# A decoder layer on one core: the first block sum of each group moved from VectorE to an accumulating DMA, weight blocks put into any free slot, and attention heads begun while the value projection still runs

## The chip, the cores and the metric

The kernel runs on one core of a Trainium2 chip. The metric is the device time of one execution in microseconds (us), less being better: the median of three runs of the kernel before is 1005.34 us.

The core's engines work side by side, each through its own list of instructions in order, and wait for one another on semaphores: TensorE multiplies matrices (PE in the profile; PEld is its loading of weights), VectorE (DVE) and ScalarE (ACT) do elementwise work, GpSimd (POOL) does a little of it and issues some transfers, and SyncE (SP) issues the rest.

## What is computed

The reference is one residual layer with four causal token mixers, for a sequence of 256 tokens and a width of 2048. Cut to what matters:

```python
h = rms_norm(x, norm_w)
p = h @ w_in                       # 2048 x 17492: z, gates, q/k/v of four mixers, indexer
o = [dsa(...), fox(...), diff(...), dilated(...)]   # four heads of 128 each
for b in range(4):
    y = o[b].reshape(1, 256, 512) * silu(z[b])
    term = sigmoid(gate[b]) * (y @ w_branch[b])     # 512 x 2048
    merged = term if b == 0 else merged + term
out = rms_norm(x + merged @ w_out, final_norm_w)    # 2048 x 2048
```

All of it is in float32. The mixers differ in their logits: dsa attends to the 64 best keys of an indexer with 16 small heads, fox adds cumulative forget gates, diff subtracts two softmax maps, and dilated merges three windows. Each head ends in a product of its probabilities with v.

## The kernel before

**Numbers.** TensorE gets each float32 operand as a high and a low part. For a weight block, ScalarE writes the high part (`whi`, `split_hi`, L194) and VectorE the low part (`wlo`, `split_lo`, L207), each for half a block at a time, and `three` multiplies high by high, low by high and high by low (L365 to L367). ScalarE runs up to `HI` = 8 such halves ahead of the products, VectorE up to `LO` = 6.

**Blocks.** Weights come from HBM in blocks of 512 rows by 512 columns (1 MB, `Raw`, tile `raw`), into six slots. Each block has a slot written down in the program and each slot its own queue (`waiting`): `free` loads the slot's next block when the low half of the last product that reads it has been written. The loads are issued on SyncE's queue.

**Groups.** `seven` multiplies two 512-column blocks of the output by a scheme with seven products, in place of eight, over the first half of the rows, and four plain products (c1a, c1b, c2a, c2b) over the second. It is called 17 times: for each of the four branches q with k, z with v, and two groups of gates; and once for the output projection (`Out`). A group's units are P1 to P7 and the four plain ones, a P unit of 12 matmuls of 128x512, a c unit of 24. Four sums of weight blocks belong to a group, made in place by `plus` (VectorE, 128x2048, L174): B12+B11, then +B22, then B21 plus that, and B11 minus that. The first is made ahead of P5, the first unit of the group (fourth in the first group and the last, which are `late`). A function `plus_dram`, which adds a block from HBM by a transfer on POOL's queue, stands in the file and isn't called.

**Order.** `units` lists all units, and the main loop writes them out one after the other: the splits that lie ahead, the unit's matmuls, its evictions (`post`), and then, at intervals, one step of every thread that is active (`run_threads`). Threads are generators for what isn't a weight product: the indexer, the transposes of q and k (`qk_thread`) and of z, and the attention heads (`head_thread`, `diff_thread`). A step is taken when the summed `cost` of units reaches `pace`: 17, or 14 in branch 2; here 12 for a P unit and 24 for a c unit. What the threads issue stands in the engines' lists at that place. The branches come in the order 3 (dilated), 2 (diff), 0 (dsa), 1 (fox). A branch's heads begin with its values in place: they start behind the unit c1b of the group of z and v, which waits for `qk`, `fox`, `const` and, for dsa, `index`. In a head, logits go through a softmax (L802), `transposed` turns the probabilities (tiles `ptp` in PSUM, `pt` in SBUF, copied by ScalarE at L813), and a product with v gives `o` (L855) or `od` (L886). A branch's product with `w_branch` (`ps_b`) waits for its four heads.

Of the kernel before, what the change touches and what calls it, by code (L numbers as in the profile page):

```python
# [20 lines left out]
KC = D // P  # L21
# [52 lines left out]
class Raw:  # L74


    def __init__(self, slot, src, k0, nk, c0, n):
        self.slot, self.src, self.k0, self.nk, self.c0, self.n = slot, src, k0, nk, c0, n
        self.tile = self.then = None
# [31 lines left out]
def body(ctx: ExitStack, tc, x, norm_w, w_in, fox_b_f, lq1, lk1, lq2, lk2, subln_w,  # L111
# [227 lines left out]
    def tok_units(src, c0, act, slots, evict, name, need=(), start=()):  # L339

        st = {}
        units = []
        nk = 4 * len(slots)
        for i, slot in enumerate(slots):
# [5 lines left out]
            units.append(Unit(Raw(slot, src, 4 * i, 4, c0, 512), mm))  # L350
# [27 lines left out]
    def T_units(c0, evict, name, slots, ps_of=main_ps):  # L378
# [3 lines left out]
        for k0 in range(0, KC, 4):  # L382
# [11 lines left out]
            units.append(Unit(Raw(slots[k0 // 4], w_in, k0, 4, c0, 512), mm))  # L394
# [40 lines left out]
    def seven(src, c1, c2, base, ev, name, need={}, start=(), late=False, s0=0):  # L435
# [5 lines left out]
        B11, B12 = Raw(0, src, s0, 4, c1, 512), Raw(1, src, s0, 4, c2, 512)  # L441
        B21, B22 = Raw(3, src, s0 + 4, 4, c1, 512), Raw(2, src, s0 + 4, 4, c2, 512)
# [30 lines left out]
        def c(k0, c0, two):  # L473
            return Unit(Raw(4 + k0 // 4 % 2, src, k0, 4, c0, 512), plain(k0, two))
# [16 lines left out]
        u1 = unit("P1", B11, product("Y", whole(0, s0), True), [read(ev.p1, "Y")])  # L491
        u3 = unit("P3", B22, product("Z", form(0, 4), not late))
        second = [lambda: plus(B12, B22), lambda: free([B22])]
        fourth = [lambda: plus(B21, B12), lambda: free([B12])]
        u6 = unit("P6", B12, product("Y", form(0, 0)), [read(ev.u2, "Y")])
        u7 = unit("P7", B11, product("Y", form(1, 0)), [read(ev.u3, "Y")], frees=[B11],
                  pre=[lambda: plus(B11, B12, ALU.subtract)])
        u2 = unit("P2", B21, product("X", whole(0, s0 + 4), True))
        u4 = unit("P4", B21, product("Y", whole(1, s0 + 4)), frees=[B21])
        c2a, c2b = c(p0, c2, "ZW"), c(p0 + 4, c2, "ZW")  # L500
        c1a, c1b = c(p0, c1, "XY"), c(p0 + 4, c1, "XY")
        c2a.need += need.get("c2a", ())
        c1b.need += need.get("c1b", ())
        c1b.post += [read(ev.c11, "X", True), read(ev.c21, "Y", True)]
        c1b.start += start
        if late:
            u5.after += second[:1]
            u3.after += second[1:]
            u6.after += fourth
            u1.cost = u2.cost = 24  # L510
            u7.post += [read(ev.c12, "Z", True), read(ev.c22, "W", True)]
            return [c2a, u1, u2, u5, u3, u6, c2b, u7, c1a, u4, c1b]
        u6.pre += second
        u2.after += fourth
        c2b.post += [read(ev.c12, "Z", True)]
        u2.post += [read(ev.c22, "W", True)]
        return [u5, u1, u3, c2a, u6, c2b, u7, u2, c1a, u4, c1b]

    class Tok:


        def __init__(self, dst, s1, s2, late=False):
            self.dst, self.s1, self.s2, self.late = dst, s1, s2, late

        def p1(self, ps):
            if self.late:
                self.d1, self.d2 = self.dst()
            nc.scalar.activation(self.d1[:, 0], ps, AF.Copy, scale=self.s1[:, 0:1])

        def p5(self, ps):  # L530
            if self.late:
                nc.scalar.activation(self.d2[:, 1], ps, AF.Copy, scale=self.s2[:, 1:2])
            else:
                self.d1, self.d2 = self.dst()
# [7 lines left out]
        def u3(self, ps):  # L542
            if self.late:
                nc.vector.scalar_tensor_tensor(self.d2[:, 1], ps, self.s2[:, 1:2],  # L544
                                               self.d2[:, 1], op0=ALU.mult, op1=ALU.subtract)
            else:
                nc.scalar.activation(self.d2[:, 1], ps, AF.Copy, scale=self.s2[:, 1:2])  # L547
# [36 lines left out]
    def qkvz_units(b, off, scale, start):  # L584
# [36 lines left out]
        def z_thread():  # L621
# [209 lines left out]

    def head_thread(b, h):
        if h == 0:
            V["yT"] = big.tile([P, 4, 2, S], F32R, name="yT", tag="y")
        for _ in range(2 * h):
            yield
# [11 lines left out]
        scaled(e, r)  # L848
        yield
# [9 lines left out]
    def diff_thread(b, h):  # L859
        if h == 0:  # L860
            V["yT"] = big.tile([P, 4, 2, S], F32R, name="yT", tag="y")
        for _ in range(2 * h):
            yield
# [15 lines left out]
        yield  # L879
        yield  # L880
        pt = transposed(e0)
        yield
# [73 lines left out]
    def branch_units(b, n):  # L956
        def ev(ps):
# [6 lines left out]
            elif n == 0:  # L964
                for i in range(2):
                    load_m(i)
        units = tok_units(w_branch[b], n * 512, lambda k: (V["yT"][:, k, 0], V["yT"][:, k, 1]),
                         ((2, 0, 1, 3) if b == LAST else (2, 4, 3, 5))[n:n + 1], ev,
                         "ps_b", need=[f"att{b}"] if n == 0 else [],
# [98 lines left out]
    def out_units(n, slots):  # L1068
        if n == 2:
# [3 lines left out]
            return tok_units(w_out, n * 512, m_act, slots, ev, "ps_o")  # L1073
# [22 lines left out]
        units = [Unit(Raw(slots[i], w_out, 4 * i, 4, n * 512, 512), mm) for i in range(4)]  # L1096
# [7 lines left out]
    misc = Unit(Raw(3, w_in, 0, KC, ((O_IK, 80), (O_FF, 4)), 84), misc_mm,  # L1104
                start=[("index", misc_thread), ("const", const_thread)])
    misc.post.append(lambda: ev_misc(misc))
    units = T_units(O_IQ, lambda ps: ev_iq(ps, 0), "ps_iq", (0, 1, 2, 3))
    units[3].start += [rms_thread]
    units += T_units(O_IQ + 512, lambda ps: ev_iq(ps, 1), "ps_iq", (4, 0, 1, 2), ps_of=att_ps)
# [170 lines left out]
```

## Time and profile before

| what | value |
|---|---|
| median of 3 runs | 1005.34 us (1004.07 to 1007.09) |
| the profiled execution | 1004.6 us, of which the span of its instructions 1002.8 |
| TensorE busy | 959.9 us, 96% of the span |
| VectorE busy | 852.9 us, 85% |
| ScalarE busy | 626.3 us, 62% |
| GpSimd busy | 50.2 us, 5% |
| mean granted clock of TensorE | 0.985 of full speed |
| moved by DMA | 195.81 MB, 195 GB/s on average |

A stretch of the span in which an engine is idle costs nothing if that engine isn't the one that the others wait for. TensorE's busy share is the first thing to look at here; its ends are modelled, so 96% isn't 96% of its best. A granted clock under 1 means that TensorE ran a part of that stretch at 1.2 GHz in place of 2.4.

### The profile page before, as it was taken

The numbers are of one execution on the slowest core, as the hardware profiler recorded it, in microseconds if no ns is written. First come the engines' busy times: TensorE is split into PE (matmuls) and PEld (weight loads), VectorE is DVE, ScalarE is ACT, GpSimd is POOL, SyncE is SP. The second block draws the span as 40 slices with busy tenths as digits, with TensorE's granted clock in tenths as the row PEclk, the third lists the DMA queues.
The fourth block names the chain that finished last, engine by engine and source line by source line (L and its number), as shares of the span: only waits on it lengthen the run. The fifth ranks groups of instructions, "written<-read, shape, count | busy, mean of one in ns | idle before, by whom it ended". The sixth has DMA issues, their size and how long they took to land.

```text
span 1002.8 us, 12075 instructions
## 1 busy us (share of the span) xinstructions
PE 959.9 (96%) x4443; PEld 790.4 (79%) x4443; DVE 852.9 (85%) x985; ACT 626.3 (62%) x828; POOL 50.2 (5%) x67
## 2 busy tenths in 40 slices
PE   9997898999999999889999999999999999999896
PEld 8876686878888887668888887788888878888676
DVE  5898899989788987789799899887998989779982
ACT  5847464796655656685456667864666787544551
POOL 2010000000000000020100000001000000010130
PEclk9999899999999999899999999999999999999998
DMA  9936355555766555337786655577756465866232
GB/s 318 298 134 196 124 168 167 169 168 184 278 225 228 197 168 168 126 126 238 223 232 202 218 168 168 168 262 208 236 201 210 164 210 187 309 232 238 86 125 84
DMA packets 100043, 195.81 MB, mean 195 GB/s; under 512 B 7811, under 2 KB 10021, under 8 KB 99600
## 3 DMA queue, kind: packets, MB, share of 16 engines
q1 hardware_dynamic: 96240, 181.06, 53.5%
q0 software_dynamic: 3712, 13.98, 5.3%
q8 instruction: 35, 0.57, 0.2%
q14 instruction: 24, 0.20, 0.1%
q10 hardware_dynamic: 32, 0.01, 0.0%
HBM read 186.61 MB, written 8.41 MB: 194 GB/s over the span
## 4 chain that ended last, share of the span: by engine, by line
PE 78%; DVE 13%; issue 4%; ACT 3%; DMA 1%; POOL 0%; ACTq 0%; POOLq 0%; DVEq 0%; SPq 0%
PE ps_g L365 9%; PE ps_g L367 9%; PE ps_g L366 9%; DVE wlo L207 6%; PE ps_zv L367 5%; PE ps_zv L365 5%; PE ps_zv L366 5%; PE ps_qk L365 5%; PE ps_qk L366 5%; PE ps_qk L367 5%; PE ps_iq L370 3%; PE ps_b L367 3%; PE ps_b L365 3%; PE ps_b L366 3%; DVE raw L174 3%
## 5 line engine op out<-in xcount | busy, mean ns | idle before, releaser
L194 ACT ACTIVATE whi<-raw 128x1024 fp32r<-128x1024 f32 (+1 forms) x439 | 448.1, 1051 | 221.3 <-DVE raw L174 70.1
L207 DVE TENSOR_TENSOR wlo<-raw,whi 128x1024 fp32r<-128x1024 f32 (+1 forms) x439 | 523.2, 1222 | 44.6 <-ACT whi L194 9.9
L174 DVE TENSOR_TENSOR raw<-raw 128x2048 f32<-128x2048 f32 x68 | 155.6, 2288 | 19.4 <-DMA raw<-in_w_in_dram 17.9
L365 PE MATMUL ps_g<-whi,hT 128*128 128x512 f32 x352 | 141.9, 403 | 0.0
L367 PE MATMUL ps_g<-wlo,hT 128*128 128x512 f32 x352 | 138.2, 393 | 0.0
L366 PE MATMUL ps_g<-whi,hT 128*128 128x512 f32 x352 | 138.1, 392 | 0.0
L365 PEld LDWEIGHTS ps_g<-whi,hT 128*128 128x128 f32 x352 | 66.7, 189 | 15.2 <-issue 1.6
L367 PEld LDWEIGHTS ps_g<-wlo,hT 128*128 128x128 f32 x352 | 66.7, 189 | 14.4
L366 PEld LDWEIGHTS ps_g<-whi,hT 128*128 128x128 f32 x352 | 66.7, 190 | 13.3
L365 PE MATMUL ps_qk<-whi,hT 128*128 128x512 f32 x176 | 69.8, 396 | 4.4 <-DVE tok L544 4.4
L367 PE MATMUL ps_zv<-wlo,hT 128*128 128x512 f32 x176 | 69.7, 396 | 3.0 <-DVE wlo L207 3.0
L365 PE MATMUL ps_zv<-whi,hT 128*128 128x512 f32 x176 | 69.7, 396 | 0.7 <-ACT v L547 0.7
L366 PE MATMUL ps_qk<-whi,hT 128*128 128x512 f32 x176 | 69.3, 394 | 0.0
L367 PE MATMUL ps_qk<-wlo,hT 128*128 128x512 f32 x176 | 69.2, 393 | 0.0
L366 PE MATMUL ps_zv<-whi,hT 128*128 128x512 f32 x176 | 69.0, 392 | 0.0
L365 PE MATMUL ps_g<-whi,sf 128*128 128x512 f32 x128 | 52.2, 408 | 0.0
L366 PE MATMUL ps_g<-whi,sf 128*128 128x512 f32 x128 | 50.3, 393 | 0.0
L367 PE MATMUL ps_g<-wlo,sf 128*128 128x512 f32 x128 | 50.3, 393 | 0.0
L365 PE MATMUL ps_b<-whi,yT 128*128 128x512 f32 x128 | 49.8, 389 | 0.0
L367 PE MATMUL ps_b<-wlo,yT 128*128 128x512 f32 x128 | 49.8, 389 | 0.0
L366 PE MATMUL ps_b<-whi,yT 128*128 128x512 f32 x128 | 49.8, 389 | 0.0
L365 PEld LDWEIGHTS ps_qk<-whi,hT 128*128 128x128 f32 x176 | 33.6, 191 | 12.4 <-DVE tok L544 4.8
(266 smaller groups left out, 1519.9 us busy)
## 6 DMA issues: line engine op xcount, KB each, us to landing
raw<-in_w_in_dram SPq DMA_DIRECT2D x132, 1024.0 KB, 5.1
raw<-in_w_branch_dram SPq DMA_DIRECT2D x16, 1024.0 KB, 5.3
raw<-in_w_out_dram SPq DMA_DIRECT2D x16, 1024.0 KB, 5.3
md<-g POOLq DMA_DIRECT2D x12, 512.0 KB, 5.3
raw<-in_w_in_dram SPq DMA_DIRECT2D x7, 512.0 KB, 9.7
xs<-in_x_dram SPq DMA_DIRECT2D x8, 256.0 KB, 7.5
mp<-md POOLq DMA_DIRECT2D x4, 512.0 KB, 3.6
xf<-in_x_dram POOLq DMA_DIRECT2D x2, 1024.0 KB, 7.8
```

The lines of the kernel that those rows point to most:

```text
L174: nc.vector.tensor_tensor(to.tile, of.tile, to.tile, op=op)
L194: nc.scalar.activation(u.parts[0][h][:, s_], raw[:, s_], AF.Copy)
L207: nc.vector.tensor_tensor(u.parts[1][h][:, s_], raw[:, s_], u.parts[0][h][:, s_].bitcast(F32), op=ALU.subtract)
L365: nc.tensor.matmul(ps, ahi, u.hi(k)[:, cols], start=first, stop=False, skip_group_check=on)
L366: nc.tensor.matmul(ps, alo, u.hi(k)[:, cols], start=False, stop=False, skip_group_check=on)
L367: nc.tensor.matmul(ps, ahi, u.lo(k)[:, cols], start=False, stop=last, skip_group_check=on)
L370: nc.tensor.matmul(ps[:m], u.hi(k)[:, j * P:j * P + m], hT[:, k0 + k].rearrange("p a s -> p (a s)"), start=k0 + k == 0, stop=False)
```

## The change

It has four parts. (1) The first sum of each group, B12+B11, is made by `plus_dram`: a transfer issued by POOL reads B11 once more from HBM and adds it to B12 in SBUF. It is issued two units behind the load of B12 (`behind`, `step_behind`), and B12's load is queued four units earlier (`lead`); P5 becomes the third unit of a group (fourth of the first). The other three sums stay on VectorE. (2) A block takes any free slot, from one queue that is sorted by the place of its first use. (3) Heads start during the group of z and v: `ready` lets the first two heads (one in branch 2) run up to their softmax ahead of the values, `values` holds their products with v back until v is there, and the group's last unit waits only for `qk`. `diff_thread` yields once more between `transposed` and the product `od`. All units of a group count 12 toward a step (24 in the output group), at a pace of 18 or 15; a group then gives (11 x 12) / 18 = 7.3 steps where it gave (7 x 12 + 4 x 24) / 17 = 10.6. (4) The order of the first and the last group changes, and the last one's c2a is put ahead of the last block of the output's third column block.

```diff
-    waiting = [deque() for _ in range(SLOTS)]
+    waiting = deque()
+    slots = deque(range(SLOTS))
+    behind = []
+    def step_behind(only=None):
+        for item in list(behind):
+            item[0] -= 1
+            if item[0] <= 0 or item[1] is only:
+                behind.remove(item)
+                item[1].then()
     def load(r, parts=1, part=None):
         if not part:
+            r.slot = slots.popleft()
...
         if r.then:
-            r.then()
+            behind.append([2, r])
     def free(raws):
         for r in raws:
-            if waiting[r.slot]:
-                load(waiting[r.slot].popleft())
+            slots.append(r.slot)
+            if waiting:
+                load(waiting.popleft())
...
         nc.vector.tensor_tensor(to.tile, of.tile, to.tile, op=op)
...
-    def seven(src, c1, c2, base, ev, name, need={}, start=(), late=False, s0=0):
+    def seven(src, c1, c2, base, ev, name, need={}, start=(),
+              order="P1 P3 P5 c2a P6 c2b P7 P2 c1a P4 c1b", s0=0):
...
         p0 = 8 - s0
-        B11, B12 = Raw(0, src, s0, 4, c1, 512), Raw(1, src, s0, 4, c2, 512)
-        B21, B22 = Raw(3, src, s0 + 4, 4, c1, 512), Raw(2, src, s0 + 4, 4, c2, 512)
...
+        B11 = Raw(src, s0, 4, c1, 512)
+        B12 = Raw(src, s0, 4, c2, 512, lead=4)
+        B21, B22 = Raw(src, s0 + 4, 4, c1, 512), Raw(src, s0 + 4, 4, c2, 512)
+        B12.then = lambda: plus_dram(B12, B11)
...
-        def unit(what, raw, mm, post=(), frees=(), loads=(), pre=()):
-            u = Unit(raw, mm, frees=frees, loads=loads, post=post, pre=pre, need=need.get(what, ()))
-            u.cost = 12
-            return u
-        u5 = unit("P5", B12, product("V" if late else "W", form(1, 4), True),
-                  [read(ev.p5, "V" if late else "W")], loads=[B12, B11, B22, B21],
-                  pre=[lambda: plus(B12, B11)])
...
-        return [u5, u1, u3, c2a, u6, c2b, u7, u2, c1a, u4, c1b]
...
+        U = {
+            "P1": Unit(B11, product("Y", whole(0, s0), True), [read(ev.p1, "Y")], frees=()),
+            "P2": Unit(B21, product("X", whole(0, s0 + 4), True), frees=()),
+            "P3": Unit(B22, product("Z", form(0, 4), not apart), frees=()),
+            "P4": Unit(B21, product("Y", whole(1, s0 + 4)), frees=[B21], loads=()),
+            "P5": Unit(B12, product(Q, form(1, 4), True), [read(ev.p5, Q)], frees=()),
+            "P6": Unit(B12, product("Y", form(0, 0)), [read(ev.u2, "Y")], frees=(), loads=()),
+            "P7": Unit(B11, product("Y", form(1, 0)), [read(ev.u3, "Y")], frees=[B11], loads=(),
+                       pre=[lambda: plus(B11, B12, ALU.subtract)]),
...
+        }
+        U["P5"].after.append(lambda: plus(B12, B22))
+        last_of("P3", "P5").after.append(lambda: free([B22]))
+        last_of("P2", "P6").after += [lambda: plus(B21, B12), lambda: free([B12])]
...
+            u.cost = 24 if s0 else 12
+        return [U[what] for what in order]
...
+            V["v of"] = b
...
-        return (seven(w_in, off, off + 512, lambda: hT, Tok(dst_qk, sc, rst, b == FIRST),
-                      "ps_qk", need={"P1": ["stack"], "P5": ["forms"]} if b == FIRST else {},
-                      start=[("qk", qk_thread)], late=b == FIRST)
+        return (seven(w_in, off, off + 512, lambda: hT, Tok(dst_qk, sc, rst), "ps_qk",
+                      start=[("qk", qk_thread)] + start, **(dict(
+                          need={"P1": ["stack"], "P3": ["forms"]},
+                          order="P1 P2 P3 P5 c2a P6 c2b P7 c1a P4 c1b") if b == FIRST else {}))
                 + seven(w_in, O_Z + b * 512, off + 1024, lambda: hT, Tok(dst_zv, rst, rst),
-                        "ps_zv", need={"c1b": ["qk", "fox", "const"] + ["index"] * (b == 0)}, start=[z_thread] + start))
+                        "ps_zv", need={"c1b": ["qk"]}, start=[("z", z_thread)]))
...
+    def ready(b, h, early):
+        while any(a[0] in ("qk", "index", "fox", "const") for a in active):
+            yield
+        if h < early:
+            for _ in range(2 * h):
+                yield
+        else:
+            while V.get("v of") != b:
+                yield
+            for _ in range(h - early):
+                yield
+                yield
+    def values(b):
+        while V.get("v of") != b or any(a[0] == "z" for a in active):
+            yield
...
         scaled(e, r)
+        yield from values(b)
         yield
...
         yield
...
         yield
+        yield from values(b)
         yield
         pt = transposed(e0)
+        yield
         yield
...
         for u in units[-22:]:
-            u.pace = 14 if b == 2 else 17
+            u.pace = 15 if b == 2 else 18
...
-    units += out_units(2, (4, 5, 2, 1))
+    two = out_units(2)
     for n in range(4):
-        units[n - 4].need.append(f"merge{n}")
-    units += seven(w_out, 0, 512, lambda: V["mT"], Out(), "ps_o", late=True, s0=8,
-                   need={"P5": ["merge3"]})
+        two[n].need.append(f"merge{n}")
+    group = seven(w_out, 0, 512, lambda: V["mT"], Out(), "ps_o", s0=8, need={"P5": ["merge3"]},
+                  order="c2a P1 P5 c2b P6 P2 P7 P3 c1a P4 c1b")
+    units += two[:3] + group[:1] + two[3:] + group[1:]
...
-    units += out_units(3, (2, 1, 0, 4))
+    units += out_units(3)
     warm = att_ps("warm")
...
-    for u in units[4:]:
-        for r in u.loads:
-            waiting[r.slot].append(r)
-    load(waiting[4].popleft())
-    load(waiting[5].popleft())
+    rest = [(i - r.lead, i, r) for i, u in enumerate(units) if i > 3 for r in u.loads]
+    waiting += [r for _, _, r in sorted(rest, key=lambda e: e[:2])]
+    load(waiting.popleft())
+    load(waiting.popleft())
...
     def high(q):
         i, h = divmod(q, 2)
         if i < len(units):
+            if any(r is units[i].raw for _, r in behind):
+                step_behind(units[i].raw)
             split_hi(units[i], h, kept(units[i]))
...
             low(2 * i + h + LO - 1)
             high(2 * i + h + HI - 1)
             u.mm(u, h)
+        step_behind()
...
```

On VectorE, where the first sums of two groups of branch 2 stood (q with k, z with v; `raw` is a block, `tok` an eviction of a product), before:

```order
L174 TENSOR_TENSOR raw_2332<-raw_2154,raw_2332 128x2048
L207 TENSOR_TENSOR wlo_2633<-raw_2513,whi_2605 128x1024
L551 SCALAR_TENSOR_TENSOR tok_2509<-ps_qk_2540,rst_109,tok_2509 128x512
L207 TENSOR_TENSOR wlo_2650<-raw_2513,whi_2619 128x1024
L174 TENSOR_TENSOR raw_2617<-raw_2593,raw_2617 128x2048
L207 TENSOR_TENSOR wlo_2663<-raw_2332,whi_2635 128x1024
L207 TENSOR_TENSOR wlo_2674<-raw_2332,whi_2654 128x1024
L207 TENSOR_TENSOR wlo_2687<-raw_2559,whi_2665 128x1024
```

and in the changed kernel, with the second sum of the group (L187) in the first row:

```order
L187 TENSOR_TENSOR raw_2369<-raw_2188,raw_2369 128x2048
L220 TENSOR_TENSOR wlo_2632<-raw_2485,whi_2604 128x1024
L552 SCALAR_TENSOR_TENSOR tok_2507<-ps_qk_2516,rst_109,tok_2507 128x512
L220 TENSOR_TENSOR wlo_2649<-raw_2485,whi_2618 128x1024
L220 TENSOR_TENSOR wlo_2661<-raw_2369,whi_2634 128x1024
L220 TENSOR_TENSOR wlo_2672<-raw_2369,whi_2653 128x1024
L220 TENSOR_TENSOR wlo_2685<-raw_2558,whi_2663 128x1024
L557 SCALAR_TENSOR_TENSOR tok_2507<-ps_qk_2537,rst_109,tok_2507 128x512
L220 TENSOR_TENSOR wlo_2696<-raw_2558,whi_2676 128x1024
L220 TENSOR_TENSOR wlo_2714<-raw_2592,whi_2687 128x1024
```

The row of the next group's first sum is gone, here and at 16 other places; the splits follow one another.

On POOL, from the last instruction that norms the input (`dg`) to the two masks of the indexer's scores (`sc0` is the first of them), before:

```order
L289 TENSOR_SCALAR dg_614<-ident_82,rst_109 128x128 x2
L321 DMA vdr_115<-vsb_771 13x383
L307 DMA bias_826<-vdr_115 128x4x256
L307 DMA mask_114<-vdr_115 128x256
L696 DMA ncd_123<-ncum_122 4x256
L763 AFFINE_SELECT sc0_125<-sc0_125 128x128
```

and in the changed kernel:

```order
L302 TENSOR_SCALAR dg_614<-ident_82,rst_109 128x128 x2
L191 DMA raw_391<-in_w_in_dram 128x4x512
L334 DMA vdr_115<-vsb_758 13x383
L191 DMA raw_786<-in_w_in_dram 128x4x512
L320 DMA bias_839<-vdr_115 128x4x256
L320 DMA mask_114<-vdr_115 128x256
L699 DMA ncd_123<-ncum_122 4x256
L191 DMA raw_1176<-in_w_in_dram 128x4x512
L766 AFFINE_SELECT sc0_125<-sc0_125 128x128
```

The accumulating transfers (L191) stand between what POOL did already; 17 rows of that kind are new.

On ScalarE, at the first transposed head of branch 2 (`g` is a gate, `lg` a head's logits), before:

```order
L194 ACTIVATE whi_3330<-raw_3157 128x1024
L194 ACTIVATE whi_3346<-raw_3003 128x1024
L571 ACT_TABLE_LOAD
L571 ACTIVATE g_3138<-g_3138 128x512
L813 ACTIVATE pt_3366<-ptp_3362 128x384
L818 ACTIVATE lg_3225<-lg_3225,sm_3227 128x128
L818 ACTIVATE lg_3225<-lg_3225,sm_3227 128x256
```

and in the changed kernel:

```order
L805 ACTIVATE lg_3401,sm_3403<-lg_3401,mx_3402 128x128
L805 ACTIVATE lg_3401,sm_3403<-lg_3401,mx_3402 128x256
L207 ACTIVATE whi_3413<-raw_3261 128x1024
L207 ACTIVATE whi_3429<-raw_3302 128x1024
L816 ACTIVATE pt_3447<-ptp_3443 128x384
L821 ACTIVATE lg_3285<-lg_3285,sm_3287 128x128
L821 ACTIVATE lg_3285<-lg_3285,sm_3287 128x256
```

The copy `pt` has no gate's table load ahead of it now. On TensorE, 12 matmuls of 128x512 stand between this head's `ptp` and its `od` before, and 36 in the changed kernel; for the other three heads of that branch 24, 24 and 12 become 36, 36 and 48. Between the last head's last transposes and the branch product stand 168, 84, 180 and 180 such matmuls before (branches 3, 2, 0, 1), and 144, 0, 120 and 120 in the changed kernel. Three heads of branch 0 and three of branch 1 now copy their `pt` in direct succession. Behind an accumulating transfer's place, 99 to 155 matmuls stand ahead of the one whose `whi` reads the sum in 16 groups, and 44 in the first. The first product of the indexer (`ps_ix`, L749) has 212 matmuls ahead of it where it had 188. ScalarE loads an activation table 30 times where it did so 24 times.

## Rows read from the trace of the kernel before

**Rows 1.** The page: busy time by engine, and the chain that ended last.
```profile
PE 959.9 (96%) x4443; PEld 790.4 (79%) x4443; DVE 852.9 (85%) x985; ACT 626.3 (62%) x828; POOL 50.2 (5%) x67
...
PE 78%; DVE 13%; issue 4%; ACT 3%; DMA 1%; POOL 0%; ACTq 0%; POOLq 0%; DVEq 0%; SPq 0%
```

**Rows 2.** Windows: length, busy PE PEld DVE ACT POOL, clock, DMA share, GB/s.
```profile
75.00:125.00 50.00, 39.40 (x181) 31.82 (x180) 44.18 (x67) 30.72 (x41) 1.89 (x3) 0.90 0.49 161
125.00:175.00 50.00, 46.38 (x210) 37.37 (x209) 49.00 (x88) 28.25 (x34) 1.69 (x2) 0.97 0.50 166
175.00:250.00 75.00, 73.00 (x340) 60.30 (x339) 68.62 (x84) 60.04 (x87) 0.00 (x0) 1.00 0.53 172
250.00:375.00 125.00, 125.00 (x560) 103.51 (x559) 106.32 (x91) 74.03 (x81) 2.96 (x5) 1.00 0.65 222
375.00:450.00 75.00, 67.04 (x292) 51.80 (x291) 58.20 (x106) 55.57 (x108) 6.54 (x8) 0.93 0.42 138
...
575.00:650.00 75.00, 71.94 (x334) 59.05 (x333) 66.99 (x89) 56.59 (x85) 0.00 (x0) 1.00 0.50 163
...
775.00:850.00 75.00, 73.90 (x344) 61.23 (x343) 66.80 (x83) 56.95 (x85) 1.08 (x2) 1.00 0.54 183
...
925.00:975.00 50.00, 44.64 (x191) 35.02 (x190) 47.20 (x41) 28.55 (x38) 11.74 (x6) 1.00 0.30 106
975.00:1002.00 27.00, 20.02 (x134) 18.38 (x132) 8.82 (x18) 3.93 (x10) 3.27 (x4) 0.92 0.21 78
```

**Rows 3.** Waits: engine, line waited for: us in total, times, longest.
```profile
ACT whi L194 <- DVE raw L174: 70.1, 27, 7.8
...
PE ps_ix L749 <- ACT ki_hi L660: 3.3, 1, 3.3
...
PE o L855 <- ACT pt L813: 6.2, 5, 2.2
...
PE od L886 <- ACT pt L813: 8.0, 2, 4.0
```

**Rows 4.** The block sums' group of instructions: busy us, mean ns | idle before.
```profile
L174 DVE TENSOR_TENSOR raw<-raw 128x2048 f32<-128x2048 f32 x68 | 155.6, 2288 | 19.4 <-DMA raw<-in_w_in_dram 17.9
```

**Rows 5.** Timeline from 403 to 410 us: start, duration, engine, line.
```profile
403.73 2.29 DVE L174 TENSOR_TENSOR raw<-raw 128x2048 f32<-128x2048 f32 x1
...
406.06 1.06 ACT L194 ACTIVATE whi<-raw 128x1024 fp32r<-128x1024 f32 x1 [1.45 <-DVE raw L174]
...
407.12 1.28 ACT L571 ACT_TABLE_LOAD   x1
...
409.48 0.49 PE L886 MATMUL od<-v,pt 128*128 128x128 f32 x2 [3.97 <-ACT pt L813]
```

**Rows 6.** DMA queues (packets, MB, share of 16 engines) and issues.
```profile
q1 hardware_dynamic: 96240, 181.06, 53.5%
q0 software_dynamic: 3712, 13.98, 5.3%
...
raw<-in_w_in_dram SPq DMA_DIRECT2D x132, 1024.0 KB, 5.1
...
md<-g POOLq DMA_DIRECT2D x12, 512.0 KB, 5.3
...
mp<-md POOLq DMA_DIRECT2D x4, 512.0 KB, 3.6
xf<-in_x_dram POOLq DMA_DIRECT2D x2, 1024.0 KB, 7.8
...
fw<-in_final_norm_w_dram POOLq DMA_DIRECT2D x1, 1024.0 KB, 11.8
```

**Rows 7.** Timeline from 53 to 66 us, POOL and ScalarE.
```profile
53.44 1.63 POOL L289 TENSOR_SCALAR dg<-ident,rst 128x128 f32<-128x128 f32 x2
...
63.06 2.00 ACT L194 ACTIVATE whi<-raw 128x1024 fp32r<-128x1024 f32 x2
```

**Rows 8.** The longest wait of POOL.
```profile
POOL md L962 <- DVE g L960: 403.2, 12, 180.2
```

More of the change, by code (lines that the diff above doesn't have):

```diff
@@ L74, with __init__ @@
 class Raw:
-    def __init__(self, slot, src, k0, nk, c0, n):
-        self.slot, self.src, self.k0, self.nk, self.c0, self.n = slot, src, k0, nk, c0, n
-        self.tile = self.then = None
+    def __init__(self, src, k0, nk, c0, n, lead=0):
+        self.src, self.k0, self.nk, self.c0, self.n, self.lead = src, k0, nk, c0, n, lead
+        self.slot = self.tile = self.then = None
 class Unit:
@@ L337, in h_act, with tok_units @@
         return hT[:, k, 0], hT[:, k, 1]
-    def tok_units(src, c0, act, slots, evict, name, need=(), start=()):
+    def tok_units(src, c0, act, evict, name, n4=4, need=(), start=()):
         st = {}
         units = []
-        nk = 4 * len(slots)
-        for i, slot in enumerate(slots):
+        nk = 4 * n4
+        for i in range(n4):
             def mm(u, h, k0=4 * i):
@@ L349, in mm @@
                     tok_mm(st["ps"][t], u, h, act, k0, nk, t)
-            units.append(Unit(Raw(slot, src, 4 * i, 4, c0, 512), mm))
+            units.append(Unit(Raw(src, 4 * i, 4, c0, 512), mm))
         units[0].need += need
@@ L376, in T_lo, with T_units @@
                          start=False, stop=k0 + k == KC - 1)
-    def T_units(c0, evict, name, slots, ps_of=main_ps):
+    def T_units(c0, evict, name, ps_of=main_ps):
         st = {}
@@ L393, in mm @@
                             between = None
[L394 removed]
+            units.append(Unit(Raw(w_in, k0, 4, c0, 512), mm))
         units[-1].post += [lambda: evict(st["ps"]), lambda: done(*st["ps"])]
@@ L473, in c @@
         def c(k0, c0, two):
-            return Unit(Raw(4 + k0 // 4 % 2, src, k0, 4, c0, 512), plain(k0, two))
+            return Unit(Raw(src, k0, 4, c0, 512), plain(k0, two))
         def read(f, bank, last=False):
@@ L492, in seven @@
[L492 to L516, printed above, removed]
-        return [u5, u1, u3, c2a, u6, c2b, u7, u2, c1a, u4, c1b]
+        def last_of(*names):
+            return U[max(names, key=order.index)]
+        Q = "V" if apart else "W"
+        U = {
[7 more added lines that the diff above has]
+                       pre=[lambda: plus(B11, B12, ALU.subtract)]),
+            "c2a": c(p0, c2, "ZW"), "c2b": c(p0 + 4, c2, "ZW"),
+            "c1a": c(p0, c1, "XY"), "c1b": c(p0 + 4, c1, "XY"),
+        }
@@ new lines, in seven @@
+        U["P5"].after.append(lambda: plus(B12, B22))
+        last_of("P3", "P5").after.append(lambda: free([B22]))
+        last_of("P2", "P6").after += [lambda: plus(B21, B12), lambda: free([B12])]
+        last_of("P3", "P6", "c2b").post.append(read(ev.c12, "Z", True))
+        last_of("P7", "c2b", "P2").post.append(read(ev.c22, "W", True))
+        U["c1b"].post += [read(ev.c11, "X", True), read(ev.c21, "Y", True)]
+        U["c1b"].start += start
+        for what, u in U.items():
+            u.need += need.get(what, ())
+            u.cost = 24 if s0 else 12
@@ L542, in u3 @@
         def u3(self, ps):
[L543 to L547, printed above, removed]
+            nc.scalar.activation(self.d2[:, 1], ps, AF.Copy, scale=self.s2[:, 1:2])
         def c12(self, ps):
@@ L834, in head_thread @@
             V["yT"] = big.tile([P, 4, 2, S], F32R, name="yT", tag="y")
-        for _ in range(2 * h):
-            yield
+        yield from ready(b, h, 2)
         ps = att_ps("lps")
@@ L861, in diff_thread @@
             V["yT"] = big.tile([P, 4, 2, S], F32R, name="yT", tag="y")
-        for _ in range(2 * h):
-            yield
+        yield from ready(b, h, 1)
         er = []
@@ L1066, in c21, with out_units @@
             out_col(ps, 1, 0, 512, 0)
-    def out_units(n, slots):
+    def out_units(n):
         if n == 2:
@@ L1072, in ev @@
                     out_col(ps[t], t, n * 512, 512, n)
-            return tok_units(w_out, n * 512, m_act, slots, ev, "ps_o")
+            return tok_units(w_out, n * 512, m_act, ev, "ps_o")
         st = []
@@ L1095, in mm @@
                 final(1, S, part)
-        units = [Unit(Raw(slots[i], w_out, 4 * i, 4, n * 512, 512), mm) for i in range(4)]
+        units = [Unit(Raw(w_out, 4 * i, 4, n * 512, 512), mm) for i in range(4)]
         units[-1].keep = True
```

25 lines of the change are left out of this document (10 added, 15 removed).

## The prediction

> **What bounds the kernel now.** The page first [rows 1]: TensorE is busy for 959.9 of 1002.8 us, and the chain that ended last lies on it for 78% and on VectorE for 13%. So TensorE is the bound, and VectorE, busy for 85%, is the one that it sometimes waits for. An average doesn't say where; the windows do [rows 2]. From 250 to 375 us, a stretch of gates, TensorE is busy for all of 125 us and gets through 560 matmuls, 0.223 us from one to the next, at a granted clock of 1.00. The heads and the start are otherwise: from 75 to 125 it is busy for 39.40 of 50 us, from 125 to 175 for 46.38, with clocks of 0.90 and 0.97, and from 375 to 450, where the heads of branch 2 run, for 67.04 of 75 at 0.93. In the first two of these VectorE is busy for 44.18 and 49.00 of 50 us: there it is the bound.
>
> What these stretches wait for is in the waits [rows 3]. TensorE waits twice, 8.0 us together, for `pt` ahead of `od`, five times, 6.2 us, ahead of `o`, and once, 3.3 us, for the indexer's key. Behind that, ScalarE's `whi` waits 27 times, 70.1 us in all and up to 7.8 us, for a block sum of VectorE: a sum takes 2.288 us, and there are 68 [rows 4]. The timeline at 403 us shows the whole chain once [rows 5]: a sum runs from 403.73 for 2.29 us, `whi` waits for it and starts at 406.06, then come a table load of 1.28 us and a gate, and only then the copy `pt` that `od` needs; TensorE has stood for 3.97 us when it goes on at 409.48.
>
> **What the change does, part by part.** The sum is made against the profiled execution, 1004.6 us (the median of three runs is 1005.34, 0.7 us above).
>
> *The sums.* VectorE loses 17 sums, 17 x 2.288 = 38.9 us. Where TensorE is at 125 of 125 us this gives nothing: VectorE has 15% of the time free there already (106.32 of 125). It gives what VectorE holds back in the other stretches. From 75 to 175 us, idle TensorE comes to (50 - 39.40) + (50 - 46.38) = 14.2 us, and the clock's loss to 0.10 x 50 + 0.03 x 50 = 6.5 us, together 20.7. Three first sums lie there, and VectorE is nearly full, so their 3 x 2.29 = 6.9 us come back whole. The wait for the indexer's key, 3.3 us, comes 24 matmuls later, 24 x 0.223 = 5.4 us of cover, and goes. With 10.2 of the 14.2 us of idleness gone, I let three quarters of the clock's loss come back, 4.9 us, since both windows' clocks fell where TensorE stood. That is 15.1 us; the bounds are 4 (half of the sums, nothing else) and 20.7. From 175 to 250 us I take 1 of 2.0 idle us. From 925 to 975, with VectorE at 47.20 of 50, one sum, 2.3 of 5.4 idle us.
>
> *The price of the transfers.* No 1 MB accumulating transfer is in this trace. The nearest [rows 6]: the two 1 MB reads on POOL's queue (`xf`) take 7.8 us from issue to landing, `fw` takes 11.8, and an accumulating write of 512 KB (`md`) 5.3 against 3.6 for a plain read of that size (`mp`), 1.7 more. Twice that on top of 7.8 is 11.2, which I take, as `xf` is the same shape of read; the bounds are 7.8 and 11.8 + 5.3 = 17. Sixteen of the 17 have 99 to 155 matmuls between their place and the first `whi` that reads them, 22 to 35 us at 0.223: hidden at either bound. Cover would be gone if POOL got to them more than 5 us late. POOL is busy for 5% [rows 1]; what stands ahead of them in its list are mostly stores that wait for an eviction of the matmuls just done. The first has 44 matmuls, 10 us. POOL is free for it when `dg` ends at 53.44 + 1.63 = 55.1 us, so it lands at 66; the `whi` of the unit that reads it now ran from 63.06 to 65.06 [rows 7]. ScalarE comes some 2 us late there, of which its lead of several halves takes in a part: 1 us of cost, 0 at the lower bound and 72 - 64 = 8 at the upper.
>
> The transfers also share engines with the loads. The loads move 181.06 MB in 53.5%, 0.30% for a MB, the queue with the accumulating stores 13.98 MB in 5.3%, 0.38% [rows 6]. So 17 x 1.05 = 17.8 MB more are 6.8% of the 16 engines, 13.5% if accumulating doubles it: 59% becomes 66 to 73%. The busiest stretch of 125 us shows 0.65 with TensorE never idle [rows 2], so a load of 5.1 us stays hidden, and I cost this at nothing. Here a rule of the Trainium skill speaks against the change: "DMA: Bandwidth & Descriptors", section "Issuing engines are not separate DMA queues", says that transfers issued by any engine run on the same 16 DMA engines and interleave, and that issuing from several engines saves only sequencer time. By that rule the sums would slow the loads, and the forecast would come to that of the third rival; no row of the trace shows a load held back by a store of POOL's.
>
> *The free slots.* A block no longer waits for the one slot that it was given. The loads of blocks other than the first two of a sum never stop TensorE in the waits, so I cost this at nothing on either side: it moves transfers that are hidden.
>
> *The heads.* In branch 2, `od` now has 36 matmuls ahead of it, 36 x 0.223 = 8.0 us, where it had 12, 2.7 us, and waited up to 4.0. Since 2.7 + 4.0 = 6.7 is under 8.0, both waits go: 8.0 us, and of the clock's loss from 375 to 450, 0.07 x 75 = 5.3, I let 4 return. That is 12 of 13.2. For branches 0 and 1, the idle time of their head stretches is 75 - 71.94 and 75 - 73.90, 4.2 us, of which I take 2.5, as softmaxes move to where TensorE has other work. What is lost: three `pt` in a row in these two branches make the first product wait for all three copies; five waits of `o` took 6.2 us, 1.24 each [rows 3], and I take a little over half of that for each of the two places, 1.5 us together (0 to 2.5). In branch 2 the last head's transposes now stand directly ahead of the branch's product, where 84 matmuls, 19 us, stood between: the chain of two VectorE operations and one of ScalarE lies open. I take 1 us, the bounds being 0 and the 4.0 of an `od` wait. Six more table loads, 6 x 1.28 = 7.7 us, lie on ScalarE, which is busy for 62%.
>
> *The sum.* 15.1 + 1 + 2.3 + 12 + 2.5 = 32.9 us off, 1 + 1.5 + 1 = 3.5 us on: 1004.6 - 29.4 = 975 us.
>
> **The rivals.** *More comes back:* all that the windows show as lost goes, 20.7 + 2.0 + 13.2 + 4.2 + 5.4 = 45.5 us, and no cost shows: 959; with the 27.0 - 20.0 = 7.0 us of the last window, whose order changes too, 952. For it: the sums stand ahead of most `whi` waits. Against: it needs every term at its bound.
>
> *Only the start pays:* the head waits don't go but move, into the rows of three copies and the open end of branch 2. Then 15.1 + 2.3 + 1 come off and 2.5 on: 989. For it: in branches 0 and 1, `o` still stands 12 matmuls behind its `pt`, as in the rows where it waited. Against: branch 2's cover triples.
>
> *The sums slow the loads:* each group's loads land a third later, 1.8 us on 5.1, and TensorE waits for that once a group, 17 x 1.8 = 31 us: about 1006, no change. It needs loads that are already late, and the DMA share of 0.65 beside a full TensorE speaks against it.
>
> *Slower:* the sums land late. POOL takes its list in order, and it waits for VectorE up to 180.2 us at a store [rows 8]; an accumulating transfer behind one starts only when that is through. The point from which it decides is 22 us from place to landing; each microsecond past it is up to 16 us, in every group but the first. At 25 us, 16 x 3 = 48 on and 29 off: 1023. Against: at 11.2 us landing, POOL may be 11 us late before anything shows.
>
> **How the numbers follow.** The forecast has a chance of 0.58, with 960 to 988 as its own range (the opening at 4 to 20.7, the costs at 3.5 to 11); more comes back 0.09; only the start 0.17; slowed loads 0.07; late sums 0.09. The range that leaves out the last two, but for their near ends, and reaches to the first rival's end is 953 to 998. A difference under 0.3%, 3 us, can't be told from no change in this kernel: faster by more than that 0.84, within it 0.07, slower 0.09.
>
> **What would show it.** Right: VectorE busy for 853 - 39 = 814 us and 51 sums; accumulating transfers that land in about 11 us, and no long wait of `whi` or TensorE for one; 75 to 175 us with under 5 us idle and a clock above 0.97; no `od` wait above 1 us; new waits of about 1 us where three copies stand in a row and at the start of branch 2's product. Wrong: `whi` waiting for a DMA in most groups (late sums), loads well above 5.1 us with TensorE waiting for whole blocks (shared engines), or a clock still near 0.9 in the start though VectorE is freer, which would say that VectorE didn't hold it back. The term that I trust least is the clock's 9 us.

## The result: 1043.84 us, slower by 3.7%

The changed kernel takes 1043.84 us (median of three, 1041.32 to 1044.16) against 1005.34: a ratio of 1.0374 (95% interval 1.0339 to 1.0409). The forecast was 975, with a range up to 998. The profiled execution's span is 1042.4 us, 39.6 more than before.

The page after, the line of busy times that answers to [rows 1], the sums that answer to [rows 4], and the queues and issues that answer to [rows 6]:

```profile
PE 973.3 (93%) x4443; PEld 799.7 (77%) x4443; DVE 822.7 (79%) x967; ACT 634.7 (61%) x834; POOL 73.0 (7%) x84
...
q1 hardware_dynamic: 96240, 181.06, 50.1%
q0 software_dynamic: 12688, 31.80, 14.9%
...
L187 DVE TENSOR_TENSOR raw<-raw 128x2048 f32<-128x2048 f32 x51 | 117.8, 2310 | 1.1
...
raw<-in_w_in_dram SPq DMA_DIRECT2D x132, 1024.0 KB, 6.4
raw<-in_w_in_dram POOLq DMA_DIRECT2D x16, 1024.0 KB, 11.3
...
mp<-md POOLq DMA_DIRECT2D x4, 512.0 KB, 8.7
```

The sums did what they were to do: 51 in place of 68, VectorE freer by 30 us (38.9 were expected), the 16 transfers from `w_in` landing in 11.3 us. TensorE makes the same 4443 matmuls. It is busy 13.4 us longer, which goes with the lower clock (0.966 on average, 0.985 before), and idle 26.2 us longer (1042.4 - 973.3 = 69.1 against 42.9). What it waits for then, as in [rows 3], with waits of VectorE and ScalarE:

```profile
PE ps_g L378 <- ACT g L540: 25.9, 6, 6.5
ACT L805 <- DVE mx L803: 25.7, 4, 10.2
...
DVE lg L800 <- PE ptp L814: 23.3, 4, 10.6
...
PE o L876 <- ACT pt L816: 14.6, 4, 6.7
...
DVE lg L798 <- PE ptp L814: 10.6, 1, 10.6
...
PE ps_qk L378 <- ACT tok L540: 6.9, 4, 4.1
```

No wait for `od` is left, as forecast. In its place stands one that the kernel before did not have: L540 is the eviction of P5 (`Tok.p5`), and TensorE waits 25.9 + 6.9 us for it ahead of a plain product. The second new thing is `o`, 14.6 us where it was 6.2, with waits of VectorE for transposes, up to 10.6 us, ahead of it. By stretch, as in [rows 2]:

```profile
75.00:125.00 50.00, 44.15 (x205) 35.66 (x203) 42.74 (x61) 29.76 (x39) 3.20 (x4) 0.93 0.63 203
125.00:175.00 50.00, 49.54 (x242) 41.45 (x241) 47.52 (x70) 34.30 (x43) 3.06 (x3) 1.00 0.67 208
175.00:250.00 75.00, 68.49 (x306) 55.72 (x305) 66.76 (x105) 52.86 (x81) 1.34 (x1) 0.95 0.57 178
...
575.00:650.00 75.00, 68.49 (x306) 56.40 (x305) 50.35 (x69) 44.79 (x63) 1.29 (x1) 0.95 0.59 191
650.00:775.00 125.00, 116.98 (x509) 96.00 (x508) 104.08 (x102) 77.19 (x91) 6.62 (x7) 0.96 0.72 215
```

The first two stretches gained: idle time went from 14.2 to 6.3 us and the clock rose from 0.90 and 0.97 to 0.93 and 1.00. From 175 us on, every stretch with heads lost. The last row was a stretch of gates with TensorE busy throughout; the heads of branch 0 now reach into it. VectorE's load isn't the cause: from 575 to 650 it is busy for 50.35 of 75 us, less than before, while TensorE stands longer.

One of the waits for P5 on the timeline (start, duration):

```profile
605.71 0.40 ACT L805 ACTIVATE lg<-lg,mx 128x128 f32<-128x128 f32 x1 [2.84 <-DVE mx L803]
...
606.71 1.28 ACT L625 ACT_TABLE_LOAD   x1
608.00 1.06 ACT L625 ACTIVATE sg<-tok 128x1024 f32<-128x1024 f32 x1
608.96 1.99 ACT L207 ACTIVATE whi<-raw 128x1024 fp32r<-128x1024 f32 x2
...
610.86 0.67 ACT L540 ACTIVATE g<-ps_g,rst 128x512 f32<-128x512 f32 x1
...
611.58 0.79 PE L378 MATMUL ps_g<-whi,hT 128*128 128x512 f32 x1 [6.51 <-ACT g L540]
```

The unit c2a adds to PSUM banks Z and W, and W is the bank that P5 wrote and that ScalarE must evict first. With P5 first, P1, P3 and the Z half of c2a stood between, 12 + 12 + 6 = 30 matmuls or 6.7 us at 0.223. With P5 third only the Z half does: 6 matmuls, 1.3 us. ScalarE had other work ahead of the eviction: here a head's exponentials, which had waited 2.84 us for VectorE, and the gate z's sigmoid with its table load; elsewhere a `whi` that waits for a block sum.

The other wait, for `o`, with VectorE's and ScalarE's part of it:

```profile
647.94 0.27 PE L814 MATMUL ptp<-ident,lg 128*128 128x128 f32 x1
...
648.25 0.29 DVE L798 TENSOR_TENSOR lg<-lps,bias 128x128 f32<-128x128 f32 x1 [10.61 <-PE ptp L814]
...
649.96 1.28 ACT L805 ACT_TABLE_LOAD   x1 [10.18 <-DVE mx L803]
...
652.15 3.88 ACT L207 ACTIVATE whi<-raw 128x1024 fp32r<-128x1024 f32 x4
656.05 1.28 ACT L580 ACT_TABLE_LOAD   x1
...
658.45 0.86 ACT L816 ACTIVATE pt<-ptp 128x384 f32<-128x384 f32 x2
...
658.98 1.22 PE L876 MATMUL o<-pt,v 128*128 128x256 f32 x2 [6.72 <-ACT pt L816]
```

The fourth head's softmax stands on VectorE for 10.61 us until a transpose is through: `lg` has three buffers, and the three heads ahead hold theirs until the values come. ScalarE's exponentials wait behind it for 10.18 us, and the copies `pt` stand behind those, behind four splits and behind two gates.

### The profile page after: what moved, and what is told of

It is laid out like the page before. It is cut to its first block, busy times and chain, and to the rows that moved or that the text cites. A ratio compares the mean times of both kernels' runs of the same rounds, so it can differ in the third digit from the quotient of the medians.

```text
span 1042.4 us, 12131 instructions
## 1 busy us (share of the span) xinstructions
PE 973.3 (93%) x4443; PEld 799.7 (77%) x4443; DVE 822.7 (79%) x967; ACT 634.7 (61%) x834; POOL 73.0 (7%) x84
## 3 DMA queue, kind: packets, MB, share of 16 engines
q0 software_dynamic: 12688, 31.80, 14.9%
## 5 line engine op out<-in xcount | busy, mean ns | idle before, releaser
L378 PE MATMUL ps_g<-whi,hT 128*128 128x512 f32 x352 | 145.9, 415 | 25.9 <-ACT g L540 25.9
L380 PE MATMUL ps_g<-wlo,hT 128*128 128x512 f32 x352 | 141.9, 403 | 0.4 <-DVE wlo L220 0.4
L379 PE MATMUL ps_g<-whi,hT 128*128 128x512 f32 x352 | 142.2, 404 | 0.0
L187 DVE TENSOR_TENSOR raw<-raw 128x2048 f32<-128x2048 f32 x51 | 117.8, 2310 | 1.1
L378 PEld LDWEIGHTS ps_g<-whi,hT 128*128 128x128 f32 x352 | 69.6, 198 | 44.2 <-ACT g L540 28.4
L380 PEld LDWEIGHTS ps_g<-wlo,hT 128*128 128x128 f32 x352 | 69.1, 196 | 16.0 <-DVE wlo L220 0.8
L379 PEld LDWEIGHTS ps_g<-whi,hT 128*128 128x128 f32 x352 | 69.4, 197 | 14.0
L191 POOL DMA_DIRECT2D raw<-in_w_in_dram x16 | 21.1, 1316 | 503.5 <-DMA raw<-in_w_in_dram 191.1
L380 PE MATMUL ps_b<-wlo,yT 128*128 128x512 f32 x128 | 49.8, 389 | 0.0
L379 PE MATMUL ps_b<-whi,yT 128*128 128x512 f32 x128 | 49.8, 389 | 0.0
## 6 DMA issues: line engine op xcount, KB each, us to landing
raw<-in_w_in_dram POOLq DMA_DIRECT2D x16, 1024.0 KB, 11.3
```

What stands on the lines that cost most here:

```text
L187: nc.vector.tensor_tensor(to.tile, of.tile, to.tile, op=op)
L191: nc.gpsimd.dma_start(to.tile.rearrange("p (k n) -> p k n", k=of.nk), of.src[of.k0 * P:(of.k0 + of.nk) * P, of.c0:of.c0 + of.n] .rearrange ...
L378: nc.tensor.matmul(ps, ahi, u.hi(k)[:, cols], start=first, stop=False, skip_group_check=on)
L379: nc.tensor.matmul(ps, alo, u.hi(k)[:, cols], start=False, stop=False, skip_group_check=on)
L380: nc.tensor.matmul(ps, ahi, u.lo(k)[:, cols], start=False, stop=last, skip_group_check=on)
```

## The experiments

Four theories: (1) P5's place next to c2a, by the bank that they share; (2) the transfers, by shared engines or by landing late; (3) the early heads, at first put down to table loads and three copies in a row; (4), from the trace, the early heads by the three `lg` buffers. Each edit is against the changed kernel unless said otherwise. The kernel before took 1004.5 to 1006.2 us beside them.

**P5 first again.**

```diff
-              order="P1 P3 P5 c2a P6 c2b P7 P2 c1a P4 c1b", s0=0):
+              order="P5 P1 P3 c2a P6 c2b P7 P2 c1a P4 c1b", s0=0):
...
```

> The changed kernel with P5 moved back to the first place in the 15 groups of the common order (P5 P1 P3 c2a ...); sums by the transfer, free slots and early heads stay. Theory 1 (P5's place): the unit c2a, which adds to P5's PSUM bank, stands 30 matmuls behind P5's last one and not 6, so TensorE no longer waits for ScalarE's eviction of P5 (ACT g, tok and v at L540: 25.9 + 6.9 + 0.5 us of idle time in the changed kernel, of which 4.1 in the first group, which keeps its order). About 29 us of idle time go, and some 8 us of the clock's loss: about 1005 us (998 to 1014). Theory 2 (the transfers slow the loads or come late) and theory 3 (the early heads) expect no more than 10 us off: 1034 or more.

Measured: 1012.53 us. 31 of the 38 us are gone. The first group keeps its order; there P5 had a bank of its own before the change and now shares W.

**P5 third, in its own bank.**

```diff
-        Q = "V" if apart else "W"
+        Q = "V"
...
```

> The changed kernel with P5 still third, but written to a PSUM bank of its own, which c2a doesn't touch; P5 is evicted twice (ScalarE, one eviction of 0.67 us more for each of 16 groups), and the eviction of P7 moves from ScalarE to VectorE. Theory 1: all 33 us of waits for L540 go, less some of the 16 x 0.67 = 11 us on ScalarE: about 1003 us (995 to 1015). If it were the order of the products as such, and not the bank that they share, this would change nothing: 1040. Theories 2 and 3: 1034 or more.

Measured: 1010.24 us, and no wait of TensorE for P5's eviction is left. So the order costs this time only because P5 and c2a share the bank. P7's eviction moved as well, but the run ahead of this one gained as much without that.

**The first sum on VectorE.**

```diff
-        B12.then = lambda: plus_dram(B12, B11)
...
-            "P5": Unit(B12, product(Q, form(1, 4), True), [read(ev.p5, Q)], frees=()),
+            "P5": Unit(B12, product(Q, form(1, 4), True), [read(ev.p5, Q)], frees=(),
+                       pre=[lambda: plus(B12, B11)]),
```

> The changed kernel with the first sum of each group back on VectorE (17 times 2.3 us) and no accumulating transfer; P5 stays third, slots and early heads stay. Theory 1: P5's waits stay and VectorE has more to do: 1044 plus 0 to 25 us, about 1052. Theory 2 (the transfers cost the time, by sharing engines with the loads or by landing late): it falls back to about 1005 to 1015. Theory 3: 1044 or more.

Measured: 1045.26 us. Theory 2 falls: without the 17 transfers the loss is the same, and the gates' waits for L540 come to 26.0 us. VectorE is busy 35.7 us longer (858.4 against 822.7), and the time doesn't show that either; TensorE waits for P5 as long in both.

**The heads late.** The third part is undone: `ready`, `values` and the further yield go, costs and paces are those of before.

> The changed kernel with its third part undone: heads begin behind the values, the group's last unit waits for qk, fox, const and index, no further yield in branch 2, costs and paces of before; P5 third, transfers and free slots stay. Theory 1: the waits for P5 stay at the most; the two waits of 6.7 us for three copies in a row go, the waits ahead of od come back (8 us): about 1036 us (1028 to 1044). Theory 3 (the early heads, with six more table loads and three copies in a row, cost the time): 1005 to 1015. Theory 2: no change.

Measured: 1035.85 us. Undoing the third part alone gains 8 us, with the waits for P5 in place.

**P5 first and heads late.** Both edits; in the first group, which keeps its order, P5 has its own bank, here and in all runs on the changed kernel below.

> The changed kernel with P5 back in the first place (in the first group, which keeps its order, P5 has a PSUM bank of its own), and with the third part undone, heads behind the values. What is left of the change: the transfers in place of 17 sums, free slots, the order of the last group. From the two runs that undid one each: 1012 less 8 of the heads less 4 of the first group gives about 1000 us. If the removed sums pay as was forecast (9 us of VectorE where it was full, and the clock): 985 to 995. If they pay nothing, as the run with sums on VectorE gave (1045 beside 1044): 1000 to 1006.

Measured: 994.89 us, a ratio of 0.9884 (0.9863 to 0.9905). Against the run before it, only P5's place and its bank in the first group differ: 1035.85 - 994.89 = 41 us. Against the first run (1012.53), with the heads early, undoing the third part now gains up to 17.6 us, where it gained 8; that first group's bank has a share in this.

**The same, first sum on VectorE.** The edit of the third experiment, and B11 loaded five units earlier.

> The same as the kernel with P5 first and late heads, but the first sum of each group on VectorE again (its block B11 loaded five units earlier, beside B12), no accumulating transfer. What is left of the change: free slots and the order of the last group. The difference of these two kernels is the worth of the transfers with P5's waits and the heads' waits out of the way. Forecast of the prediction: VectorE's sums cost 9 us or more, so 9 to 15 us slower than with the transfers. Rival: VectorE's time isn't what TensorE waits for, 0 to 3 us.

Measured: 1002.93 us, 0.9983 (0.9974 to 0.9992): 8.0 us more than with the transfers, a little under what was expected. Both kernels in one stretch, the one with transfers first:

```profile
75.00:125.00 50.00, 43.86 (x215) 36.01 (x216) 45.54 (x70) 33.60 (x46) 3.75 (x5) 0.97 0.63 203
```

```profile
75.00:125.00 50.00, 40.73 (x196) 32.95 (x195) 44.38 (x64) 29.72 (x40) 1.89 (x3) 0.93 0.54 182
```

3.1 us less idle and 2 us of clock come from this stretch. It isn't a sum on VectorE that TensorE stands for there. The same wait in both, again with the transfers first:

```profile
94.76 0.50 PE L378 MATMUL ps_qk<-whi,sf 128*128 128x512 f32 x1 [2.15 <-DVE tok L553]
```

```profile
91.02 1.06 ACT L207 ACTIVATE whi<-raw 128x1024 fp32r<-128x1024 f32 x1 [6.95 <-DMA raw<-in_w_in_dram]
...
95.37 2.35 DVE L220 TENSOR_TENSOR wlo<-raw,whi 128x1024 fp32r<-128x1024 f32 x2
97.64 0.75 DVE L553 SCALAR_TENSOR_TENSOR tok<-ps_qk,rst,tok 128x512 f32<-128x512 f32 x1
...
98.44 0.80 PE L378 MATMUL ps_qk<-whi,sf 128*128 128x512 f32 x1 [5.08 <-DVE tok L553]
```

A `whi` waits for its block's load; the splits behind it, the low parts and the eviction on VectorE come later by that, and TensorE stands 2.9 us longer. Why the load comes late isn't shown; the edit queues B11's loads earlier, too. Over the whole run ScalarE's `whi` waits 22.4 us for loads from `w_in`, against 2.1 us with the transfers, and for block sums 49.2 against 49.8. So 8.0 us is the worth of the transfers together with the order of loads that each kernel has; how much of it is VectorE's time isn't shown. What then remains of the change, free slots with their order of loads and the first and last groups' order, is 0.2%.

**P5 first, the copies `pt` apart.** Early heads; the second and third head go on one and two steps later when the values come.

> The changed kernel with P5 first (as in the kernel with late heads), heads early as in the change, but the second and third head of a branch other than diff stay one and two steps behind the first when the values come, so that their three copies pt don't stand in a row. If the two waits of 6.7 us ahead of o come from the three copies, they go: 1012 less 4 of the first group less 13: about 996 us (990 to 1002). If they come from the four splits, the table load and the two gates that stand ahead of them, one wait of 4 to 5 us stays in each branch: about 1003.

Measured: 1017.37 us, a miss:

```profile
DVE lg L813 <- PE ptp L827: 19.6, 3, 9.8
...
PE o L891 <- ACT pt L829: 17.5, 4, 6.8
```

With single copies, the waits ahead of `o` are up to 6.8 us still, and VectorE still waits for transposes up to 9.8 us. So it isn't the copies in a row, and this led to theory 4.

**Kernel before, P5 third.** The edit is to the kernel before.

```diff
-        return [u5, u1, u3, c2a, u6, c2b, u7, u2, c1a, u4, c1b]
+        return [u1, u3, u5, c2a, u6, c2b, u7, u2, c1a, u4, c1b]
...
```

> The kernel before with one thing changed: P5 third (P1 P3 P5 c2a ...) in the 16 groups of the common order other than the first; sums on VectorE, fixed slots, late heads. Theory 1: this alone costs what P5's waits cost in the changed kernel, 29 us idle and some 8 of clock, less what the early heads add to them: about 1033 us (1022 to 1043). If it took the transfers, the slots or the early heads as well: 1005 to 1012.

Measured: 1014.98 us, a miss: 10 us where 28 were expected. In this edit the second sum is made ahead of P5's low part, so that this part is computed from the wrong block; the time is read for the order alone.

**The same, the sum behind P5's low part.** Kernel before with the edit above and:

```diff
-        u6.pre += second
+        u5.after += second
```

> The kernel before with P5 third in the 16 groups of the common order, and the second sum (B12 + B22) made when P5's low part has been written, as in the changed kernel; VectorE's sums, fixed slots and late heads stay. In the run that had P5 third and this sum ahead of P5's low part, 10 us were lost. Theory: the sum now stands directly ahead of the high part of P6 on ScalarE, and P5's eviction behind that, so c2a waits in most groups: 1033 us (1024 to 1043). If the place of the sum doesn't matter: 1012 to 1018.

Measured: 1033.34 us. With this order, and the second sum behind P5's low part as in the changed kernel, the kernel before loses 27 us: neither transfers nor slots nor early heads are needed. Its waits, and those of the run ahead of it:

```profile
PE ps_g L365 <- ACT g L533: 24.2, 7, 9.2
...
PE ps_zv L365 <- ACT v L533: 4.6, 4, 3.7
```

```profile
PE ps_g L365 <- ACT g L533: 14.6, 6, 5.4
```

Here L533 is P5's eviction. The bank makes TensorE wait for it; how long goes with what ScalarE does ahead. With the sum directly ahead of P6's high part, ScalarE's `whi` waits 37 times, 98.4 us in all, for a sum, against 27 times and 75.3 us with the sum a step earlier.

**The fourth head waits.** P5 first, heads early, and in `head_thread`:

```diff
         yield from ready(b, h, 2)
+        while h == 3 and V.get("pt of") != b:
+            yield
...
         pt = transposed(e)
+        V["pt of"] = b
```

> The changed kernel with P5 first (own bank in the first group), heads early, and one more rule: the fourth head of branches 3, 0 and 1 begins its logits only when the first head has been transposed. The theory after the trace: there are three buffers lg; the early heads hold theirs until the values come, so the fourth head's softmax on VectorE waits up to 10.6 us for the first head's transposes on TensorE, ScalarE's exponentials wait behind it, and the copies pt behind those: the two waits of 6.7 us ahead of o. If so, both go, with the clock's loss there (0.93 and 0.95 in 575 to 650 and 775 to 850, 9 us): 1012 less 4 of the first group less 13 to 20: about 993 us (985 to 1000). If it were the copies in a row or the table loads, it stays above 1005.

Measured: 990.55 us, 0.9861 (0.9841 to 0.9881). No product waits for `pt` any more, and VectorE's longest wait of `lg` for a transpose is 2.9 us. Against the first run, P5 first with early heads, this is 22.0 us (1012.53 - 990.55), of which the first group's bank has a part: P5's wait there was 3.5 us. Theory 4 holds, and the rest of theory 3 falls: this run makes the same 30 table loads as the changed kernel.

**Heads late, `od` a step later.** The kernel of 994.89 us with one `yield` more between `transposed` and `od`.

> The kernel with P5 first and late heads (994.9 us), with one thing of the third part back: the further yield between the transposes and od in branch 2, so that od has a step more of matmuls ahead of it. Forecast of the prediction for this term: the two waits ahead of od (7.4 us in that kernel) go, and some of the clock's 5 us from 375 to 450: 985 us (981 to 989). Rival: the wait moves behind the branch's last head, to the start of its product: 993 to 996.

Measured: 985.86 us, 0.9808 (0.9795 to 0.9821), the fastest of all. From 375 to 450 us, without the yield and with it:

```profile
375.00:450.00 75.00, 67.59 (x297) 53.46 (x297) 57.75 (x105) 54.19 (x104) 9.54 (x9) 0.93 0.46 142
```

```profile
375.00:450.00 75.00, 71.81 (x328) 56.68 (x327) 60.77 (x108) 55.18 (x104) 9.87 (x9) 0.98 0.52 167
```

4.2 us less idle and 0.05 x 75 = 3.8 us of clock.

## Why the prediction was wrong

The step that failed is one that the prediction did not take: it priced the sums, the transfers, the slots and the heads, and gave no line to P5's move to third place, which the change names. It treated that as part of "the sums". The move takes 24 matmuls out from between P5 and the product that needs P5's bank, and it put P6's high part and its sum next to P5's eviction on ScalarE. In the kernel before alone it costs 27 us; in the changed kernel 31 (heads early, without the first group) or 41 (heads late, with the first group's bank). None of the rivals held it either; the one that ended slower, late sums, was a wrong mechanism.

- **The sums.** 18.4 us were taken for the three stretches, and 8.0 were measured between two kernels that differ in the sums and in the order of loads. So the size was too large, and the mechanism, that VectorE's 6.9 us at the start come back whole, isn't shown: where these two kernels differ most, TensorE stood for a late load. In the changed kernel the gain doesn't show: 1043.84 us with the transfers, 1045.26 without, TensorE waiting for P5 in both.
- **The transfers.** 11.3 us to landing against 11.2, and over all 17 the source line's view gives, with the durations of the issue (ns, least, median, most) and who waited for one (us, times):

```profile
L191 POOL DMA_DIRECT2D raw<-in_w_in_dram x16: 1281/1312/1387, 55.5 to 822.9; - x16
...
  ACT whi L207: 1.8, 1
...
DMA to landing us min/median/max: 8.3/11.4/13.5
```

  One wait of 1.8 us, in the first group, where 1 was taken. That 11.2 came out so well has luck in it: the price of accumulating was taken from `mp`, and `mp` takes 8.7 us in the changed kernel where it took 3.6. The rivals of late sums and of slowed loads fall, though loads do land later (6.4 us against 5.1): without the transfers the time is 1045.26 us, no faster, and with P5 first and heads late it is slower, 1002.93 against 994.89.
- **The free slots** were costed at about nothing; no run has them alone, and with the order of the first and last groups they are 0.2%.
- **`od` in branch 2.** 12 us were taken; 9.0 were measured by the yield alone. The waits fell from 7.4 to 0.2 us.
- **The early heads.** The forecast took 2.5 us off and put 1.5 on for three copies in a row. Moving the copies apart took no wait away. What costs is a resource that the prediction did not look at: three `lg` buffers for four heads that now hold theirs longer, 22 us between the runs of 1012.5 and 990.6, the first group's bank included. And without that stall early heads are still not ahead of late ones (990.55 against 985.86, with `od` later in both).
- **The start.** 15.1 us were taken from 75 to 175; idle time and clock there gave 7.9 + 3.0 = 10.9, and 6.3 us stay idle where under 5 was to be the sign.

So of the terms that were priced, the sums and `od` came out smaller than taken, the transfers and slots near what was taken, and the early heads with the other sign; the sum failed on these heads and on the move that was absent. One after the other, each the difference of two neighbouring runs, the parts are 1005 - 2 (slots, orders) - 8 (sums with their loads) - 9 (`od`) + 5 (early heads) + 22 (`lg`, the first group's bank) + 31 (P5) = 1044. They add up because the runs form a chain; in another order the parts differ, as P5's 31 and 41 show. The stated range doesn't follow from its own terms either: the opening at 20.7 with costs of 3.5 gives 970, and at 4 with 11 it gives 994, not 960 to 988. Not tried: a fourth `lg` buffer.

## What to carry to other kernels

When a step moves in a hand-written order, look for everything that it shared with its old neighbours: the PSUM bank that a later product adds to, the eviction that must come between, and what stands ahead of that eviction on its engine; count the matmuls between the two before and after. When work is begun earlier, ask which buffers it holds longer, and who asks for the next one: an engine that runs its list in order stands still for all that is behind. And a gain can be real and invisible until another wait is gone; undo the parts singly and in pairs, and look in the trace whether the two kernels differ where the part acts.

## What was not expected of the hardware

An accumulating transfer of 1 MB held POOL's list for about 1.3 us at its issue, and landed in 8.3 to 13.5 us. The queue with the sums took 14.9% of the 16 engines for 31.80 MB, so the 17.8 MB more cost about 0.55% for each MB against 0.38 for what that queue moved before [rows 6], between the two bounds given. And stalls of 5 to 7 us came with more than themselves: in the changed kernel TensorE's 4443 matmuls took 13.4 us longer, at a mean granted clock of 0.966 in place of 0.985, on top of the 26.2 us more in which it stood.
